# An attention stage between dense projections: where the next unit's rows are split, where dense weights are split, and which comes first where two units meet

## The chip, the cores and the metric

The kernel runs on one core of a Trainium2 chip. The metric is the device time of one execution in microseconds (us). The kernel before takes 1624.2 us, the median of three runs (1623.47 to 1624.24).

## What is computed

The reference is one inference step of a one-layer encoder. A prompt of 1024 rows and eight samples of 16 rows each, all of width 1024, are normalised and projected to queries, keys, values and gates. Two attention branches follow, each with 8 query heads of width 64:

```python
def band_attention(q, k, v, bias, valid, sink):
    s = jnp.einsum("bqhgd,bkhd->bhgqk", q, k).astype(jnp.float32) * (HEAD_DIM ** -0.5) + bias
    s = jnp.where(valid, s, NEG_INF)
    m = jnp.max(s, axis=-1, keepdims=True)
    ...
        p = jnp.exp(s - m)
        denom = jnp.sum(p, axis=-1, keepdims=True) + jnp.exp(sk - m)
    ...
    w = (p / denom).astype(v.dtype)
    return jnp.einsum("bhgqk,bkhd->bqhgd", w, v)
```

Branch A looks back over two chunks of 64 rows, has two key heads and a learned sink in the denominator; branch B looks back over eight chunks and has eight key heads and no sink. The sample rows attend to a cache of 128 earlier rows and to themselves. After it come the output projections, the gates, a merge projection and a gated feed-forward layer with a short causal convolution, with norms between. New keys and values are outputs as well.

## The kernel before

The program goes through stages: the input projections, the attention stage, the output projections and the merge, and the two halves of the feed-forward layer. Only the attention stage concerns the change. It is the second `with ExitStack() as ph` block of `encoder_step` (from L519), and in the trace it lies at about 295 to 580 us. Matrix products in full precision are made of three products of rounded parts: an operand x is split in a high part (ScalarE, a copy to the rounded type) and a low part (x minus the high part, on VectorE or GpSimd).

**Units.** The stage has eight units `u`, two heads each: 0 to 3 of branch A (shared keys and values, at most 256 keys a block), 4 to 7 of branch B (own keys and values, at most 640 keys a block). A unit's rows are 1152 wide (1024 of the prompt, 128 of the samples) and lie in DRAM; `fetch(u)` (L638) loads them with `rows` (L580, the DMA is L583) into one of two buffers (pool `rawp`). For a unit of branch A that is q alone; for branch B it is k, q and v. Then `q_done` (L599) and `k_done` (L610) split them by `split_rows` (L586) in two halves of 512 columns: the high part on ScalarE (L591), the low part on VectorE (L593 for k, L595 for q). `v_done` (L618) transposes v on TensorE (L625, L631), and VectorE and ScalarE copy the transposes to SBUF (L627, L629, L633). A raw buffer is free when all of its readers are done, and the next load waits for that on SP's queue.

**Steps.** A unit has five steps: prompt blocks 0 and 1, the samples, prompt blocks 2 and 3. A prompt step is `scores` (L670): six pairs of matmuls and more (L697, tile `s`, the two heads on two halves of TensorE's rows), a reduction with the bias and the minimum (L700, VectorE), Exp with its sum (L705, ScalarE), a reciprocal (L718) and the norms (L722, VectorE). The step after it runs `transposes` of its probabilities (L739, tile `pt` in PSUM; the copies `pk` are L741 on VectorE and L743 on ScalarE, by turns) and then `values` (L754, tile `o`; copied by L756 to `oo`, stored by L757). A sample step has its own scores (L783, L784, tile `sss`), reduction (L791), norms (L799, and L802 into `pm`), transposes (L810, L811, tile `ts`), a copy `pcs` (L813) and values (L820, L825). So at each moment a step's scores stand beside the transposes of the step before; where units meet, the scores of block 0 of unit u stand beside the transposes of block 3 of unit u − 1.

**Dense work between.** TensorE is filled up with dense projections: ten weight tiles (`dense_tiles`), each of three groups of 24 matmuls of 128x384 (L117 to L119 in `mm3`, tile `d`), copied by ScalarE to `gt` (L574) and stored (L575). `weight_tile` (L106) loads a tile's weights (L108) and splits them: high part on ScalarE (L101), low part on GpSimd (L104).

**Order.** The program is traced step by step; `spread` (L861) puts pieces of the dense work between the items of a step:

```python
items = [step(sc), step(tr, 2), step(tr, 2), rest(sc), step(tr, 2), rest(tr), lates]
```

`sc` are the scores, `tr` the transposes of the step before, `lates` the transposes of the samples' results (L833). The `fetch` of the next unit is traced ahead of the sample step (`i == 2`). A scheduler then sets the order on each engine, which is near to the order of tracing but not the same. PSUM has three pools of two buffers each: `d`; the scores and sample scores; and all the transposes together with `o`. A transpose therefore waits for the copy of the tile two before it.

Of the kernel before, what the change touches and what calls it, by code (L numbers as in the profile page):

```python
# [13 lines left out]
AF = mybir.ActivationFunctionType  # L14
ALU = mybir.AluOpType
# [12 lines left out]
GW = T // NG  # L28
# [24 lines left out]
def encoder_step(ctx, tc, x, w_in, w_o, w_out, w_upg, w_down, kc, vc, state_conv, conv_w, conv_b,  # L53
                 sink, sink_rows, t5t, onehot, relrev, g_pre_mix, g_post_mix, g_pre_ffn, g_post_ffn,
                 y, ka_new, va_new, kb_new, vb_new, conv_new):
    nc = tc.nc
# [49 lines left out]
    def weight_tile(src, name, hi_engine="scalar", lo_engine="gpsimd"):  # L106
        raw = wr.tile([P, KD, P], F32, name=f"{name}r", tag="wr")
        nc.sync.dma_start(raw[:], src)  # L108
        sp = ws.tile([P, 2, KD, P], F32R, name=f"{name}s", tag="ws")
        split_w(raw, sp, hi_engine, lo_engine)  # L110
        return sp
# [51 lines left out]
    with ExitStack() as ph:  # L163
# [100 lines left out]
        with ExitStack() as pre:  # L264
# [12 lines left out]
            for tb in range(NT):  # L277
# [3 lines left out]
                if tb == 1:  # L281
                    box = wraw.tile([P, 2, KD, P], F32, name="iwh0", tag="uw")
# [236 lines left out]
    with ExitStack() as ph:  # L519
# [35 lines left out]

        def dense_pieces(col):

            box = {}

            def run(g):  # L560
                if g == 0:
                    box["w"] = weight_tile(w_in[col], f"w{col}")
                w, c = box["w"], slice(g * GW, (g + 1) * GW)
                ps = psd.tile([P, GW], F32, name=f"d{col}_{g}", tag="d")
                for k in range(0, KD, 2):
                    mm3(ps[:], w, [xk[k // 4][:, j, :, c] for j in range(2)], k % 4, 2, start=k == 0,
                        stop=k == KD - 2, wk0=k)
                    if k < KD - 2:
                        yield
                gt = gst.tile([P, GW], F32, name=f"gt{col}_{g}", tag="gt")  # L570
                if col == dense_tiles[-1] and g == NG - 1:
                    nc.vector.tensor_copy(gt[:], ps[:])
                else:
                    nc.scalar.activation(gt[:], ps[:], AF.Copy)  # L574
                nc.sync.dma_start(in_dr[col][:, c], gt[:])  # L575
                yield

            return [lambda g=g: run(g) for g in range(NG)]
# [57 lines left out]
        def fetch(u):  # L636

            un = units[u]  # L638
            if u < 4:
                if u == 0:  # L640
                    rows(4, "ka", k_done(shared_a, "a", ka_new, 896))
                rows(u, f"q{u}", q_done(un, u))
            else:
                p = u - 4
                rows(10 + p, f"k{u}", k_done(un, f"{u}", kb_new[p], 512))
                rows(6 + p, f"q{u}", q_done(un, u))
                rows(14 + p, f"v{u}", v_done(un, f"{u}", vb_new[p], 512))

        def kv(u):
            return shared_a if u < 4 else units[u]  # L650
# [19 lines left out]
        def scores(st, u, sb):  # L670

            un, k = units[u], kv(u)
            st.name, st.u, st.sb = f"{u}_{sb}", u, sb
            nb = 2 if u < 4 else 5
            w = nb * P
            if sb == 0:
                un.bt = [setup_head(u, h) for h in range(2)]
            st.m = sm.tile([P, 2, 2, 2], F32, name=f"m{st.name}", tag="m")
            st.d = sm.tile([P, 2, 2], F32, name=f"dn{st.name}", tag="dn")
            st.p, st.k0 = [], []  # L680
            for i in range(2):
                j = 2 * sb + i
                kb = min(j + 1, nb)
                k0 = j + 1 - kb
                n = kb * P
                nch = 2 if n > 512 else 1
                cw = n // nch
                p = [pp.tile([P, 640], F32, name=f"p{st.name}_{i}_{h}", tag="p", bufs=8) for h in range(2)]
                least = [nsink[:, head_id(u, h):head_id(u, h) + 1] if u < 4 else BIG for h in range(2)]
                for c in range(nch):  # L690
                    ps = pss.tile([P, 2, 512], F32, name=f"s{st.name}_{i}_{c}", tag="s")
                    ks = slice(k0 * P + c * cw, k0 * P + (c + 1) * cw)
                    qs = slice(j * P, (j + 1) * P)
                    for t, (a, b) in enumerate(((0, 0), (1, 0), (0, 1))):
                        for h in range(2):
                            r = slice(h * HD, (h + 1) * HD)
                            nc.tensor.matmul(ps[:, h, 0:cw], un.q[a][r, qs], k.k[b][r, ks], start=t == 0, stop=t == 2)  # L697
                    for h in range(2):
                        m = st.m[:, c, h, i:i + 1]
                        nc.vector.tensor_tensor_reduce(p[h][:, c * cw:(c + 1) * cw], ps[:, h, 0:cw],  # L700
                                                       un.bt[h][:, w - n + c * cw:w - n + (c + 1) * cw], 1.0,
                                                       least[h], ALU.add, ALU.min, m)
                        least[h] = m
                for h in range(2):
                    nc.scalar.activation(p[h][:, 0:n], p[h][:, 0:n], AF.Exp, bias=least[h], scale=-1.0,  # L705
                                         accum_out=st.d[:, h, i:i + 1])
                st.p.append(p)
                st.k0.append(k0)
                if i == 0 and nch > 1:
                    yield  # L710
            yield
            if u < 4:
                e = sm.tile([P, 2, 2], F32, name=f"se{st.name}", tag="se")
                for h in range(2):
                    hid = head_id(u, h)
                    nc.scalar.activation(e[:, h], st.m[:, 0, h], AF.Exp, bias=sinkb[:, hid:hid + 1])
                nc.vector.tensor_tensor(st.d[:], st.d[:], e[:], op=ALU.add)
            nc.vector.reciprocal(st.d[:], st.d[:])  # L718
            for i in range(2):
                n = (2 * sb + i + 1 - st.k0[i]) * P  # L720
                for h in range(2):
                    nc.vector.tensor_scalar(st.p[i][h][:, 0:n], st.p[i][h][:, 0:n], st.d[:, h, i:i + 1], None,  # L722
                                            op0=ALU.mult)

        def transposes(st):

# [113 lines left out]

            later.append(late)

        later = []
        dense_tiles = [12, 16, 8, 13, 17, 9, 24, 32, 25, 33]
        pieces = []
        for col in dense_tiles:
            pieces += dense_pieces(col)

# [22 lines left out]
        for u in range(8):  # L871
            n = pieces_per_unit[u]
            dense, pieces = pieces[:n], pieces[n:]
            quanta = 4 * len(dense)
            dense = stream(dense)
            order = [("p", 0), ("p", 1), ("s", None), ("p", 2), ("p", 3)]
            share = [3, 5, 8, 12, 16] if u < 4 else [3, 6, 9, 13, 17]
            done = 0
            for i, (kind, sb) in enumerate(order):
                st = Step()  # L880
                st.kind = kind
                if i == 2 and u < 7:
                    fetch(u + 1)
                if u == 0 and i == 1:
                    rows(5, "va", v_done(shared_a, "a", va_new, 896))
                sc = scores(st, u, sb) if kind == "p" else sample_scores(st, u)
                tr = iter(())
                if prev is not None:
                    tr = transposes(prev) if prev.kind == "p" else sample_transposes(prev)

                def step(it, n=1):
                    return lambda: [next(it, None) for _ in range(n)]

                def rest(it):
                    return lambda: [None for _ in it]

                def lates():
                    for f in later:
                        f()
                    later.clear()  # L900

                items = [step(sc), step(tr, 2), step(tr, 2), rest(sc), step(tr, 2), rest(tr), lates]
                upto = quanta * share[i] // share[-1]
                spread(items, dense, upto - done)
                done = upto
                if prev is not None:
                    values(prev) if prev.kind == "p" else sample_values(prev)
                prev = st
            for _ in dense:
                pass  # L910
# [117 lines left out]
    with ExitStack() as ph:  # L1028
# [89 lines left out]
        for i, tb in enumerate(order):  # L1118
            g, c = tb // 3, (tb % 3) * P
# [12 lines left out]
            st = xp.tile([P, 4], F32, name=f"str{tb}", tag="st")  # L1132
# [240 lines left out]
    with ExitStack() as ph:  # L1373
# [167 lines left out]
        box = {"n": 0}  # L1541
# [15 lines left out]
        for g in range(2):  # L1557
# [39 lines left out]
            p5, n, _ = stepper("p5", pairs, xb, ex, False, True)  # L1597
# [4 lines left out]
            p3, n, _ = stepper("p3", pairs, xb, ex, False, False, True)  # L1602
# [94 lines left out]
```

## Time and profile before

| | |
|---|---|
| median of three runs | 1624.2 us |
| profiled execution | 1624.3 us |
| its span on the chip | 1622.5 us |
| TensorE's granted clock over the span | 0.998 |
| input projections, 0 to 294.7 us: TensorE busy | 284.52 us |
| attention stage, 294.7 to 580 us: TensorE busy | 277.41 of 285.3 us |
| the same: VectorE, ScalarE, GpSimd busy | 205.80, 163.65, 33.81 us |
| after 580 us: TensorE busy | 1024.78 of 1042.5 us |

The profile comes from one execution. PE is TensorE, PEld its loads of weights, DVE VectorE, ACT ScalarE, POOL GpSimd, SP the queue that issues the DMAs. A row of the timeline has the start, the duration, the engine, the line, the operation, what it writes and reads, and how many instructions the row holds; in brackets is the idle time of the engine ahead of it, and what released it. A duration of several instructions goes from the start of the first to the end of the last.

### The profile page before, as it was taken

The numbers are of one execution on the slowest core, as the hardware profiler recorded it, in microseconds if no ns is written. First come the engines' busy times: TensorE is split into PE (matmuls) and PEld (weight loads), VectorE is DVE, ScalarE is ACT, GpSimd is POOL, SyncE is SP. The second block draws the span as 40 slices with busy tenths as digits, with TensorE's granted clock in tenths as the row PEclk, the third lists the DMA queues.
The fourth block names the chain that finished last, engine by engine and source line by source line (L and its number), as shares of the span: only waits on it lengthen the run. The fifth ranks groups of instructions, "written<-read, shape, count | busy, mean of one in ns | idle before, by whom it ended". The sixth has DMA issues, their size and how long they took to land.

```text
span 1622.5 us, 27938 instructions
## 1 busy us (share of the span) xinstructions
PE 1586.7 (98%) x10891; PEld 1465.6 (90%) x10891; DVE 1104.8 (68%) x2055; ACT 726.9 (45%) x1428; POOL 213.5 (13%) x287
## 2 busy tenths in 40 slices
PE   8999999999999999999999999999999999999998
PEld 6999999878788789988798999999999998888886
DVE  6976544677677755453499866676666767955987
ACT  7521233666555554332463344444444445434353
POOL 1000000211110003410002211221111211000002
PEclk9999999999999999999999999999999999999999
DMA  8654321754443265352155322122221218053023
GB/s 277 212 184 151 111 102 63 232 174 153 152 155 120 63 198 174 117 204 91 65 179 147 105 69 82 56 82 79 71 82 61 77 63 357 1 217 114 1 83 151
DMA packets 93045, 205.94 MB, mean 127 GB/s; under 512 B 19321, under 2 KB 42793, under 8 KB 92914
## 3 DMA queue, kind: packets, MB, share of 16 engines
q1 hardware_dynamic: 92640, 203.35, 36.6%
q8 instruction: 85, 1.39, 0.4%
q0 software_dynamic: 272, 0.81, 0.1%
q14 instruction: 46, 0.38, 0.1%
q10 hardware_dynamic: 2, 0.00, 0.0%
HBM read 147.61 MB, written 61.24 MB: 129 GB/s over the span
## 4 chain that ended last, share of the span: by engine, by line
PE 84%; DVE 6%; ACT 4%; DMA 3%; issue 2%; SPq 0%; POOL 0%; DVEq 0%; POOLq 0%; ACTq 0%
PE x L143 17%; PE z L143 8%; PE x L1479 8%; PE ix L143 7%; PE p L1479 6%; PE iz L143 4%; PE y L143 4%; PE o L754 2%; PE r L1127 2%; PE r L1129 2%; PE r L1128 2%; PE mp L965 2%; PE mp L967 2%; PE mp L966 2%; PE d L117 2%; PE d L119 2%
## 5 line engine op out<-in xcount | busy, mean ns | idle before, releaser
L143 PE MATMUL x<-xot,s 128*128 128x288 f32 x1152 | 158.2, 295 | 2.8 <-DVE s L1084 1.6
L143 PEld LDWEIGHTS x<-xot,s 128*128 128x128 f32 x1152 | 155.0, 188 | 3.4 <-DVE s L1084 1.9
L1479 PE MATMUL x<-wbp,zap 128*128 128x512 f32 x576 | 135.3, 389 | 0.0
L1479 PEld LDWEIGHTS x<-wbp,zap 128*128 128x128 f32 x576 | 108.1, 188 | 22.4
L1083 ACT ACTIVATE s<-uw 128x512 fp32r<-128x512 f32 x96 | 60.2, 627 | 102.7 <-issue 41.7
L705 ACT ACTIVATE p<-p,m 128x256 f32<-128x256 f32 (+4 forms) x128 | 74.8, 586 | 59.5 <-DVE m L700 59.5
L1479 PE MATMUL p<-wbp,zap 128*128 128x512 f32 x432 | 100.6, 389 | 0.0
L1479 PEld LDWEIGHTS p<-wbp,zap 128*128 128x128 f32 x432 | 81.0, 188 | 17.1 <-ACT yacc L1489 0.3
L1284 DVE SCALAR_TENSOR_TENSOR wk<-w,cw,wk 128x448 f32<-128x448 f32 (+1 forms) x144 | 86.2, 635 | 2.1 <-ACT wk L1282 1.2
L1084 DVE TENSOR_TENSOR s<-uw,s 128x512 fp32r<-128x512 f32 x96 | 66.8, 697 | 28.4 <-ACT s L1083 28.1
L1084 DVE TENSOR_TENSOR a<-uw,a 128x512 fp32r<-128x512 f32 x62 | 42.9, 692 | 62.7 <-ACT a L1083 61.5
L143 PE MATMUL z<-xot,a 128*128 128x288 f32 x576 | 80.9, 295 | 0.6 <-DVE a L1084 0.6
L143 PE MATMUL x<-xob,s 128*128 128x288 f32 x576 | 81.0, 295 | 0.3 <-DVE wk L1243 0.3
L143 PE MATMUL z<-xot,s 128*128 128x288 f32 x576 | 80.7, 295 | 0.0
L143 PEld LDWEIGHTS z<-xot,a 128*128 128x128 f32 x576 | 78.1, 188 | 0.9 <-DVE a L1084 0.9
L143 PEld LDWEIGHTS x<-xob,s 128*128 128x128 f32 x576 | 78.1, 188 | 0.7 <-DVE wk L1243 0.6
L143 PE MATMUL ix<-t,s_i 128*128 128x256 f32 (+1 forms) x576 | 78.1, 294 | 0.0
L143 PEld LDWEIGHTS z<-xot,s 128*128 128x128 f32 x576 | 78.1, 188 | 0.0
L143 PEld LDWEIGHTS ix<-t,s_i 128*128 128x128 f32 x576 | 76.7, 187 | 0.0
L176 ACT ACTIVATE s_i<-iw 128x512 fp32r<-128x512 f32 x48 | 30.0, 630 | 84.2 <-PE ix L143 40.7
L739 PE MATMUL pt<-ident,p 128*128 128x128 f32 x360 | 56.9, 282 | 8.4 <-ACT pk L743 5.5
L143 PE MATMUL x<-xob,a 128*128 128x288 f32 x456 | 63.9, 295 | 0.0
(638 smaller groups left out, 3838.5 us busy)
## 6 DMA issues: line engine op xcount, KB each, us to landing
uw<-in_w_upg SPq DMA_DIRECT2D x53, 512.0 KB, 3.7
iw<-in_w_in SPq DMA_DIRECT2D x24, 512.0 KB, 3.8
gg<-in_dr SPq DMA_DIRECT2D x16, 576.0 KB, 3.7
z_dr<-wk SPq DMA_DIRECT2D x23, 256.0 KB, 2.1
in_dr<-gt SPq DMA_DIRECT2D x30, 192.0 KB, 1.9
z_dr<-wk SPq DMA_DIRECT2D x23, 224.0 KB, 1.9
xt<-in_x SPq DMA_DIRECT2D x9, 512.0 KB, 7.8
oT<-o_dr SPq DMA_DIRECT2D x8, 576.0 KB, 5.1
```

What stands on the lines that cost most here:

```text
L117: nc.tensor.matmul(ps, w[:, 0, a], xg[0][:, b], start=start and k == 0, stop=False)
L119: nc.tensor.matmul(ps, w[:, 1, a], xg[0][:, b], start=False, stop=stop and k == nk - 1)
L143: nc.tensor.matmul(ps, w[:, i, k], right(j, c, k), start=first and n == 0, stop=last and n == len(todo) - 1, skip_group_check=True)
L705: nc.scalar.activation(p[h][:, 0:n], p[h][:, 0:n], AF.Exp, bias=least[h], scale=-1.0, accum_out=st.d[:, h, i:i + 1])
L739: nc.tensor.transpose(pt[:, h * nb + b], st.p[i][h][:, c:c + P], ident[:])
L754: nc.tensor.matmul(ps[r, c], k.vs[:, kb, r], p[h], start=n == 0, stop=n == len(st.pv) - 1)
L965: nc.tensor.matmul(ps[:], self.sp[:, 0, k], oT[k][:, 0, c], start=k % 4 == 0, stop=False)
L966: nc.tensor.matmul(ps[:], self.sp[:, 0, k], oT[k][:, 1, c], start=False, stop=False)
L1083: split["left"] = nc.scalar.activation(sp[:, 0], src, AF.Copy)
L1084: split["low"] = nc.vector.tensor_tensor(sp[:, 1], src, fr(sp[:, 0]), op=ALU.subtract)
L1284: nc.vector.scalar_tensor_tensor(out, src(t), cw[:, f, t:t + 1], out, op0=ALU.mult, op1=ALU.add)
L1479: nc.tensor.matmul(ps, z[:, i, k, c], w[:, j, k], start=first and n == 0, stop=last and n == 2, skip_group_check=True)
```

## The change

There are three edits, all in the attention stage. No instruction is added or left out.

1. `dense_pieces`: the weights of a dense tile are loaded and split where group 2 of the tile before it is traced, and no longer where its own group 0 is. The first tile's weights are traced ahead of all units.
2. The `fetch` of the next unit is traced at the same place, but inside `tc.issue_after` of two instructions: on ScalarE its instructions stand behind the last Exp of step 1, on VectorE behind the last norm of step 1. Both are recorded in the dictionary `scored`.
3. Where units meet (`i == 0`, for u from 1 to 4) the first two items change places: two transposes of the unit before are traced ahead of the first scores.

```diff
         def dense_pieces(col):
 
-            box = {}
-
             def run(g):
-                if g == 0:
-                    box["w"] = weight_tile(w_in[col], f"w{col}")
-                w, c = box["w"], slice(g * GW, (g + 1) * GW)
+                if g == 2:
+                    following = dense_tiles[dense_tiles.index(col) + 1:]
+                    if following:
+                        dense_w[following[0]] = weight_tile(w_in[following[0]], f"w{following[0]}")
+                w, c = dense_w[col], slice(g * GW, (g + 1) * GW)
...
                 for h in range(2):
-                    nc.scalar.activation(p[h][:, 0:n], p[h][:, 0:n], AF.Exp, bias=least[h], scale=-1.0,
-                                         accum_out=st.d[:, h, i:i + 1])
+                    scored["high"] = nc.scalar.activation(p[h][:, 0:n], p[h][:, 0:n], AF.Exp, bias=least[h], scale=-1.0,
+                                                          accum_out=st.d[:, h, i:i + 1])
...
-                    nc.vector.tensor_scalar(st.p[i][h][:, 0:n], st.p[i][h][:, 0:n], st.d[:, h, i:i + 1], None,
-                                            op0=ALU.mult)
+                    scored["low"] = nc.vector.tensor_scalar(st.p[i][h][:, 0:n], st.p[i][h][:, 0:n], st.d[:, h, i:i + 1],
+                                                            None, op0=ALU.mult)
...
-        later = []
+        later, scored = [], {}
         dense_tiles = [12, 16, 8, 13, 17, 9, 24, 32, 25, 33]
         pieces = []
+        dense_w = {dense_tiles[0]: weight_tile(w_in[dense_tiles[0]], f"w{dense_tiles[0]}")}
...
                 if i == 2 and u < 7:
-                    fetch(u + 1)
+                    with tc.issue_after(scored["high"].ins), tc.issue_after(scored["low"].ins):
+                        fetch(u + 1)
...
                 items = [step(sc), step(tr, 2), step(tr, 2), rest(sc), step(tr, 2), rest(tr), lates]
+                if i == 0 and 0 < u < 5:
+                    items[0], items[1] = items[1], items[0]
```

## The prediction

> **What bounds the kernel now.** The page comes first: its top line, the engines' busy time and the chain that ended last.
>
> ```profile
> span 1622.5 us, 27938 instructions
> ...
> PE 1586.7 (98%) x10891; PEld 1465.6 (90%) x10891; DVE 1104.8 (68%) x2055; ACT 726.9 (45%) x1428; POOL 213.5 (13%) x287
> ...
> PE 84%; DVE 6%; ACT 4%; DMA 3%; issue 2%; SPq 0%; POOL 0%; DVEq 0%; POOLq 0%; ACTq 0%
> ```
>
> TensorE is the bound: 35.8 us of the whole span are not matmul. The change touches only the attention stage, so the windows (20 us each, 295 to 575 us) and TensorE's waits in that stage come next.
>
> ```profile
> 395.00:415.00 20.00, 17.60 (x151) 15.07 (x150) 15.20 (x51) 11.68 (x39) 4.52 (x7) 1.00 0.50 148
> ...
> sum 280.00, PE 272.11 PEld 226.37 DVE 201.28 ACT 160.92 POOL 33.81; mean PE 19.44 PEld 16.17 DVE 14.38 ACT 11.49 POOL 2.41
> ```
>
> ```profile
> PE pt L739 <- ACT pk L743: 2.7, 6, 0.7
> PE pt L739 <- DVE pk L741: 2.4, 1, 2.4
> PE o L754 <- ACT pk L743: 1.3, 3, 0.6
> ```
>
> The second column is TensorE's busy time. Only 7.9 us of the 280 are idle, and one window holds 2.4 of them. So the change can win some 8 us in this stage, and whatever it adds to TensorE's own stream is paid in full. The waits are on copies out of PSUM ahead of transposes. The timeline shows them where unit 1 meets unit 2 (PE row, and what released it):
>
> ```profile
> 352.30 0.60 PE L739 MATMUL pt<-ident,p 128*128 128x128 f32 x4
> ...
> 352.69 0.40 ACT L705 ACTIVATE p<-p,m 128x128 f32<-128x128 f32 x1 [0.96 <-DVE m L700]
> ...
> 353.47 0.57 ACT L743 ACTIVATE pk<-pt 128x512 f32<-128x512 f32 x1
> ...
> 354.10 0.44 PE L739 MATMUL pt<-ident,p 128*128 128x128 f32 x2 [0.67 <-ACT pk L743]
> ```
>
> The first transposes are done at 352.9, but their copy stands behind two Exps on ScalarE and starts at 353.47; the last pair waits 0.67 for the PSUM tile. Units 0/1 and 2/3 meet in the same way. Where 3 and 4 meet it is worse:
>
> ```profile
> 410.11 2.68 POOL L104 TENSOR_TENSOR w9s<-w9r,w9s 128x1024 fp32r<-128x1024 f32 x1 [1.27 <-issue]
> ...
> 413.26 0.28 DVE L700 CUSTOM_DVE_ANT_0 p<-s,bt 128x128 f32<-128x128 f32 x1
> ...
> 414.84 0.44 PE L739 MATMUL pt<-ident,p 128*128 128x128 f32 x2 [2.40 <-DVE pk L741]
> ...
> 416.04 1.41 PE L754 MATMUL o<-pk,vsa 128*64 128x256 f32 x12 [0.59 <-ACT pk L743]
> ```
>
> ```profile
> L595 DVE SCALAR_TENSOR_TENSOR q4l<-q4raw,q4h x2: 692/692/693, 375.3 to 379.3; 128x512 fp32r<-128x512 f32 x2
> L595 DVE SCALAR_TENSOR_TENSOR q5l<-q5raw,q5h x2: 682/1782/2882, 409.9 to 410.5; 128x512 fp32r<-128x512 f32 x2
> ```
>
> (minimum, median, maximum in ns). One half of q5l takes 2.88 us, from 410.5 to 413.3, instead of 0.69; GpSimd's w9s runs from 410.11 to 412.79. Everything behind it on VectorE starts at 413.26: unit 4's reductions, then the copy that the transposes wait for. By the Trainium skill ("SBUF — State Buffer", section "SBUF: two separate sides"), a VectorE operation with two SBUF inputs and a GpSimd one that reads SBUF exclude each other for a whole instruction; this row fits that. After the gap the granted clock (the figure before the last two) falls:
>
> ```profile
> 416.00:417.00 1.00, 0.96 (x10) 0.82 (x12) 0.76 (x4) 0.25 (x1) 0.00 (x0) 0.83 0.91 349
> 417.00:418.00 1.00, 1.00 (x10) 0.67 (x8) 0.42 (x1) 0.00 (x0) 0.00 (x0) 0.50 1.05 424
> 418.00:419.00 1.00, 1.00 (x10) 0.90 (x8) 0.25 (x1) 0.00 (x0) 0.00 (x0) 0.50 0.98 393
> 419.00:420.00 1.00, 1.00 (x7) 0.35 (x4) 0.80 (x4) 0.58 (x2) 0.00 (x0) 0.50 0.94 353
> ```
>
> That costs 0.17 + 3 × 0.5 = 1.7 us more.
>
> **The change, part by part.** Weight tiles (traced at group 2 of the tile before): ScalarE's halves L101 keep their places in its order; on GpSimd w9s and w32s only pass some memsets and a kn copy. I cost it at nothing; no wait for weights is in the list above.
>
> The swap shows on TensorE where units 1 and 2 meet (u=2's names; p_3 and pt_3 are unit 1's last step, the last number is a serial). Before:
>
> ```order
> L697 MATMUL s_0_1_0_4165<-kal,q2h 128x256 x2
> L739 MATMUL pt_3_6_4176<-ident,p_3_0_0_4050 128x128
> L739 MATMUL pt_3_6_4176<-ident,p_3_1_0_4063 128x128
> L739 MATMUL pt_3_6_4176<-ident,p_3_0_1_4051 128x128
> L739 MATMUL pt_3_6_4176<-ident,p_3_1_1_4064 128x128
> L739 MATMUL pt_3_5_4183<-ident,p_3_0_0_4050 128x128
> ```
>
> After:
>
> ```order
> L739 MATMUL pt_3_6_4145<-ident,p_3_1_1_4069 128x128
> L697 MATMUL s_0_0_0_4169<-kah,q2h 128x128
> L739 MATMUL pt_3_5_4152<-ident,p_3_0_0_4055 128x128
> L739 MATMUL pt_3_5_4152<-ident,p_3_0_1_4056 128x128
> L697 MATMUL s_0_0_0_4169<-kah,q2h 128x128
> ```
>
> The transposes now precede the scores, so their copies precede the Exps, and eleven score matmuls cover the copy: the three waits of 0.67 go (−2.0). One matmul of a pair now stands alone between transposes.
>
> Where 3 and 4 meet, on VectorE (p_0 are unit 4's first probabilities). Before:
>
> ```order
> L756 COPY oo_2_5044<-o_2_5037 128x256
> L595 SCALAR_TENSOR_TENSOR q5l<-q5raw,q5h 128x512 x2
> L700 ISA p_0_0_0_5057,m_0_5055<-s_0_0_0_5059,bt_0_5047 128x128
> L700 ISA m_0_5055 128x1
> L700 ISA p_0_0_1_5058,m_0_5055<-s_0_0_0_5059,bt_1_5051 128x128
> ```
>
> After:
>
> ```order
> L756 COPY oo_2_5049<-o_2_5042 128x256
> L741 COPY pk_3_5_5060<-pt_3_5_5059 128x256
> L700 ISA p_0_0_0_5074,m_0_5072<-s_0_0_0_5076,bt_0_5064 128x128
> L700 ISA m_0_5072 128x1
> L700 ISA p_0_0_1_5075,m_0_5072<-s_0_0_0_5076,bt_1_5068 128x128
> ```
>
> q5l is gone to unit 4's sample step and what meets w9s now reads PSUM, so 2.40 + 0.59 of idle time and the 1.7 of low clock go: −4.7. Three smaller waits stand later. Two are for ScalarE's copies, which came late behind k6, q6 and k7, q7, split at the ends of units 4 and 5 before and in their middle after:
>
> ```profile
> 455.91 0.66 PE L739 MATMUL pt<-ident,p 128*128 128x128 f32 x4 [0.27 <-ACT pk L743]
> ...
> 498.97 0.66 PE L739 MATMUL pt<-ident,p 128*128 128x128 f32 x4 [0.28 <-ACT pk L743]
> ...
> 529.52 0.79 PE L739 MATMUL pt<-ident,p 128*128 128x128 f32 x3 [0.34 <-DVE p L722]
> ```
>
> The third waits on VectorE's norms, which stand behind a copy for the output projection (L941) before and ahead of it after. All three go: −0.9. The gains sum to 2.0 + 4.7 + 0.9 = 7.6.
>
> What it adds on TensorE. In units 3 to 6 the next unit's v transposes fall among split scores (unit 4, after):
>
> ```order
> L697 MATMUL s_2_0_1_5373<-k4h,q4l 128x320 x2
> L625 MATMUL vt_0_5233<-ident,v5raw 128x128 x4
> L625 MATMUL vt_1_5239<-ident,v5raw 128x128 x4
> L697 MATMUL s_2_0_1_5373<-k4l,q4h 128x320 x2
> L631 MATMUL vt_s<-ident,v5raw 128x128
> ```
>
> Before, the v transposes stood at the first sample scores. Over the stage the order counts 27 more changes between tilings (154 to 181) and 10 more split pairs. A change's price is a run's first pair of scores against the next:
>
> ```profile
> 357.05 0.39 PE L697 MATMUL s<-kah,q2h 64*128 64x256 f32 x2
> ...
> 357.28 0.28 PE L697 MATMUL s<-kah,q2l 64*128 64x256 f32 x2
> ...
> 357.39 0.28 PE L697 MATMUL s<-kal,q2h 64*128 64x256 f32 x2
> ```
>
> 0.23 against 0.11: 0.12 for a change, and 0.11 for the second slot of a split pair. 27 × 0.12 + 10 × 0.11 = +4.3. The bounds are 0 (some changes fall in waits) and 5.5.
>
> Waits it adds. The sample step's reductions (L791) now stand behind the next unit's q halves on VectorE. The last pm pieces of units 1 and 2 against the transposes that need them (pm's four pieces in one row, from the first's start to the last's end):
>
> ```profile
> 337.15 0.94 DVE L802 TENSOR_SCALAR pm<-ps,dns 32x16 f32<-32x16 f32 x4
> ...
> 340.49 0.27 PE L811 MATMUL ts<-ident,pm 128*128 128x128 f32 x1
> ...
> 366.96 0.94 DVE L802 TENSOR_SCALAR pm<-ps,dns 32x16 f32<-32x16 f32 x4
> ...
> 368.64 0.27 PE L811 MATMUL ts<-ident,pm 128*128 128x128 f32 x1
> ```
>
> In unit 2 the slack is 368.64 − 367.90 = 0.74, and two halves of q3l take 1.3 (0.69 each, overlapping a little): a wait of 0.5. In unit 1 the slack is 340.49 − 338.09 = 2.4. There the reductions stood ahead of four norms of step 1 and o_0's copy before, and stand behind them and q2l after: 1.1 + 0.4 + 1.3 = 2.8, so 0.4 of wait. k4l's halves leave the same step, which could give that back. Together +0.9, between 0 and 2. In units 3 to 6 the sample transposes move later in TensorE's order too, behind the v transposes, so I put nothing there.
>
> The raw loads: v5raw now waits on SP's queue for the slot that k5's second half frees. Their times to landing:
>
> ```profile
> L583 SPq DMA_DIRECT2D v5raw<-in_dr x1: 320/320/320, 409.5 to 409.5; - x1
> ...
> DMA to landing us min/median/max: 3.7/4.2/5.6
> ```
>
> The copy of o out of PSUM, and two dense matmuls in a row:
>
> ```profile
> 409.51 0.42 DVE L756 COPY oo<-o 128x256 f32<-128x256 f32 x1
> ```
>
> ```profile
> 354.55 0.34 PE L118 MATMUL d<-xk,w8s 128*128 128x384 f32 x1
> ...
> 354.73 0.34 PE L119 MATMUL d<-xk,w8s 128*128 128x384 f32 x1
> ```
>
> In unit 4 the slot is free some 1.2 us after o_0 ends (its copy 0.42, then the second half of k5l 0.69). From o_0 to vt_0 TensorE has sixteen sample scores, 18 dense matmuls and five pairs of scores: about 0.9 + 18 × 0.17 + 1.0 = 5.0 us. A landing at 4.2 makes it wait 1.2 + 4.2 − 5.0 = 0.4, with the queue 0.5; at 3.7 nothing, at 5.6 1.9. For v4 to v7: 4 × 0.5 = +2.0, between 0 and 7.6. Behind vt_0 queue the transposes of the last step.
>
> **The sum**: −7.6 + 4.3 + 0.9 + 2.0 = −0.4. The profiled run took 1624.3, 0.1 above the median of 1624.2; so 1623.8. A measurement can tell 0.2%, 3.2 us.
>
> **The rivals.** *Faster, 1618.9 (0.30)*: waits stay hidden, since dense matmuls reach over them, and only half the changes cost: −7.6 + 2.2 = −5.4. For it: the 2.4 us of unit 1's slack, and the 3.7 of the quickest load. Against: TensorE is busy 97% in the stage and hides nothing of its own.
>
> *Slower, late raw loads, 1629.4 (0.15)*: v4 to v7 land after 5.6 us, as the slowest did: 4 × 1.4 more than forecast. TensorE begins to wait above 3.8 us to landing (1.2 + 3.8 = 5.0), and the sum is over 0.2% slower above 5.1. For it: two raw loads and two stores of raw rows now follow each other closely on that queue. Against: the median is 4.2.
>
> *Slower, full drains, 1629.7 (0.08)*: each change of tiling lets the matmul in flight end, 0.34 for a dense one, not 0.12: 27 × 0.22 = +5.9. The Trainium skill ("TensorEngine Tiling (Array Packing)", section "Key Properties") says that changing the tiling mode drains TensorE. The rows of 357.05 show that a change is not free, but at a third of that price.
>
> That the change does nothing is out for two parts of three, as the rows of order show; the weight part is that case.
>
> **How the numbers follow.** Forecast 0.47, within 3.2 us either way; faster 0.30; slower 0.15 + 0.08 = 0.23. The range takes the faster case's 1618.9 and the late loads' 1629.4, rounded outward.
>
> **What would show it.** Right: no idle over 0.3 us at the four meetings of units, q5l's halves both at 0.7, granted clock 1.00 from 410 to 425, VectorE's pm releasing ts in units 1 and 2, DMA v raw releasing vt in units 3 to 6. Wrong: an idle stretch over 1 us anywhere else in the stage, another VectorE operation beside GpSimd's L104 stretched to over 2 us, or score runs that begin at 0.11.

## The result, and the profile after

The changed kernel takes 1634.3 us (median of six runs, 1633.5 to 1638.9), the kernel before 1624.2 in the same runs: a ratio of 1.0065 (95% interval 1.0049 to 1.0082). That is 10 us slower, where 1623.8 us with a range to 1629.5 had been forecast.

The page first, as before: the span, TensorE, and the chain.

```profile
span 1637.2 us, 27945 instructions
...
PE 1597.5 (98%) x10891; PEld 1471.6 (90%) x10891; DVE 1105.7 (68%) x2055; ACT 727.7 (44%) x1428; POOL 213.3 (13%) x287
...
PE 84%; DVE 5%; ACT 3%; DMA 2%; issue 1%; POOL 0%; DVEq 0%; SPq 0%; POOLq 0%; ACTq 0%
```

TensorE's busy time rose by 10.8 us for the same 10891 matmuls: much of the loss is not idle time but slower matmuls. The spans themselves can't be subtracted. This execution took 1638.9 us, and 4.2 us of its excess lie at 68 to 76 us and 1.6 at 824 us, outside the attention stage: a wait of 3.4 us on ScalarE in the input projections (1.4 before), and a wait of 1.9 us that both kernels have in the feed-forward part, were each followed by a stretch at half clock here. So what follows goes by the stage: from its first dense matmul to the start of the last dense group it takes 308.8 us, against 300.4 before, 8.4 more. Of these, 7.0 are busy time of TensorE (the first figure behind the comma; the kernel before first):

```profile
294.83:595.25 300.42, 289.71 (x2511) 241.12 (x2510) 213.25 (x754) 169.93 (x478) 33.81 (x51) 0.99 0.45 144
```

```profile
299.04:607.88 308.84, 296.68 (x2512) 243.95 (x2510) 213.91 (x754) 170.48 (x478) 33.51 (x51) 0.99 0.43 140
```

TensorE's waits in the stage:

```profile
PE vt L625 <- DMA v7raw<-in_dr: 2.3, 1, 2.3
PE o L754 <- ACT pk L743: 2.0, 3, 0.7
PE vt L625 <- DMA v5raw<-in_dr: 1.6, 1, 1.6
PE vt L625 <- DMA v6raw<-in_dr: 1.4, 1, 1.4
PE pt L739 <- DVE vs L627: 1.3, 1, 1.3
PE pt L739 <- ACT pk L743: 1.3, 5, 0.4
```

The wait of 2.4 us on VectorE's copy where units 3 and 4 meet is gone. In its place TensorE waits three times for v's raw rows, and once for the copy of v's transposes.

**Unit 4, where v5 comes late.** The timeline of TensorE, VectorE and SP's queue, from the norms of step 1 on:

```profile
426.58 1.54 DVE L722 TENSOR_SCALAR p<-p,dn 128x384 f32<-128x384 f32 x4
...
426.99 0.87 PE L754 MATMUL o<-pk,vs 128*64 128x256 f32 x8
...
428.64 0.41 DVE L756 COPY oo<-o 128x256 f32<-128x256 f32 x1
428.98 0.68 DVE L593 TENSOR_TENSOR k5l<-k5raw,k5h 128x512 fp32r<-128x512 f32 x1
...
429.69 0.32 SPq L583 DMA_DIRECT2D v5raw<-in_dr  x1
...
434.46 0.76 PE L625 MATMUL vt<-ident,v5raw 128*128 128x128 f32 x5 [1.62 <-DMA v5raw<-in_dr]
```

o_0 ends at 427.86, but the norms run to 428.12, and k5's low half, held behind them, ends at 429.66. Only then is the slot free and the load issued; it lands 4.7 us later.

**Unit 5, where a tiny operation takes 2.3 us.** GpSimd's split of a weight tile, and pm's last four pieces on VectorE:

```profile
478.85 2.36 POOL L104 TENSOR_TENSOR w32s<-w32r,w32s 128x1024 fp32r<-128x1024 f32 x1 [20.82 <-ACT w32s L101]
478.91 3.10 DVE L802 TENSOR_SCALAR pm<-ps,dns 32x16 f32<-32x16 f32 x4
479.57 1.09 PE L625 MATMUL vt<-ident,v6raw 128*128 128x128 f32 x8 [1.40 <-DMA v6raw<-in_dr]
...
482.87 0.69 DVE L627 COPY vs<-vt 128x512 f32<-128x512 f32 x1
...
483.61 0.66 PE L739 MATMUL pt<-ident,p 128*128 128x128 f32 x4 [1.32 <-DVE vs L627]
```

Four pieces of pm take 0.94 elsewhere; here they take 3.10. VectorE comes late to v6's transposes, and they hold the PSUM tile that TensorE wants. Then the clock, in windows of 1 us (the figure before the last two):

```profile
485.00:486.00 1.00, 0.70 (x5) 0.44 (x4) 0.10 (x1) 1.00 (x3) 0.00 (x0) 0.80 0.94 384
486.00:487.00 1.00, 1.00 (x6) 0.72 (x4) 0.00 (x0) 0.54 (x3) 0.03 (x1) 0.50 0.24 55
487.00:488.00 1.00, 1.00 (x7) 0.62 (x8) 0.44 (x2) 0.39 (x1) 0.92 (x2) 0.50 0.02 2
488.00:489.00 1.00, 1.00 (x6) 0.62 (x8) 0.89 (x4) 0.00 (x0) 0.10 (x1) 0.50 0.00 0
...
530.00:531.00 1.00, 1.00 (x5) 0.72 (x5) 0.93 (x2) 0.23 (x1) 0.00 (x0) 0.50 0.74 275
531.00:532.00 1.00, 1.00 (x5) 0.90 (x5) 0.70 (x4) 0.96 (x2) 0.00 (x0) 0.50 0.16 23
532.00:533.00 1.00, 1.00 (x6) 1.00 (x5) 0.00 (x0) 0.34 (x3) 0.00 (x0) 0.50 0.18 26
533.00:534.00 1.00, 1.00 (x7) 0.80 (x5) 0.37 (x1) 1.00 (x2) 0.00 (x0) 0.80 0.96 283
```

Twice TensorE runs at half clock, 1.7 us lost each time: after the waits of unit 5 and after the 2.3 us of unit 6.

**Units 1 to 3, where the swap gives little.** The three waits of 0.67 where units meet are gone, and three of 0.65 to 0.67 stand at o_0, a step later, where there was none in unit 1 before and 0.33 and 0.34 in units 2 and 3. So 0.7 us of waits are won, not 2.0. Unit 2 before, and unit 1 after:

```profile
360.92 0.87 PE L754 MATMUL o<-pk,vsa 128*64 128x256 f32 x8 [0.33 <-ACT pk L743]
```

```profile
333.14 0.39 PE L697 MATMUL s<-kah,q1h 64*128 64x256 f32 x2
...
336.69 0.57 ACT L743 ACTIVATE pk<-pt 128x512 f32<-128x512 f32 x1
...
337.32 0.87 PE L754 MATMUL o<-pk,vsa 128*64 128x256 f32 x8 [0.65 <-ACT pk L743]
```

From the first score of block 1 to o_0 it is 337.32 − 333.14 = 4.18 us. Before it was 333.25 − 329.07 = 4.18 as well: the chain through the reductions, four Exps and the copy behind them has its own length, and what TensorE does not fill of it, it waits. (In units 2 and 3 the chain grew from 3.87 to 4.20: VectorE's reductions begin 1.0 us after the first score and no longer 0.67, since the norms of the step before and o's copy, which stand ahead of them, end later.)

The table puts it together: us between the first scores of block 1 in one unit and in the next, read from the timelines (the last line but one from unit 7 to the start of the last dense group), for the two kernels and for the ten of the next section.

| | before | after | e1 | e2 | e3 | e4 | e5 | e6 | e7 | e8 | e9 | e10 |
|---|---|---|---|---|---|---|---|---|---|---|---|---|
| unit 1 to 2 | 28.0 | 28.6 | 28.6 | 28.3 | 28.6 | 28.6 | 28.7 | 28.6 | 28.0 | 28.0 | 28.7 | 28.0 |
| 2 to 3 | 28.1 | 28.6 | 28.4 | 28.2 | 28.6 | 28.6 | 28.6 | 28.6 | 28.1 | 28.1 | 28.6 | 27.8 |
| 3 to 4 | 32.2 | 31.3 | 31.7 | 30.7 | 31.2 | 31.0 | 31.2 | 30.7 | 29.4 | 30.0 | 31.0 | 29.7 |
| 4 to 5 | 44.2 | 45.3 | 43.0 | 47.0 | 46.9 | 43.3 | 47.0 | 48.6 | 43.4 | 43.0 | 43.4 | 43.4 |
| 5 to 6 | 43.1 | 48.5 | 43.1 | 47.3 | 43.1 | 43.3 | 44.9 | 50.4 | 43.0 | 43.0 | 43.3 | 43.3 |
| 6 to 7 | 44.1 | 48.1 | 43.9 | 47.7 | 44.0 | 47.7 | 46.1 | 46.4 | 44.3 | 44.0 | 45.6 | 46.5 |
| 7 to the end | 46.5 | 44.3 | 46.0 | 45.1 | 47.8 | 43.9 | 46.0 | 44.6 | 44.6 | 44.6 | 44.3 | 49.3 |
| whole stage | 300.4 | 308.8 | 299.0 | 308.3 | 304.2 | 300.4 | 306.4 | 311.8 | 295.2 | 295.4 | 299.1 | 302.4 |

Units 5 and 6 lose 5.4 and 4.0 us: all of the loss and more. The stage end wins 2.2, which the moved pieces don't explain: before, a copy for the last transposes stood on ScalarE behind a split that waited for its load; in the later stage of the changed kernel it had landed. (In e8, which moves nothing there, the row is 44.6 as well.) Before:

```profile
587.42 1.16 ACT L940 ACTIVATE oT<-oT 128x1152 fp32r<-128x1152 f32 x1 [2.62 <-DMA oT<-o_dr]
588.49 0.58 ACT L743 ACTIVATE pk<-pt 128x512 f32<-128x512 f32 x1
...
589.12 0.44 PE L739 MATMUL pt<-ident,p 128*128 128x128 f32 x2 [2.31 <-ACT pk L743]
```

A second table divides the same stage: TensorE's idle time, what the clock took (half of each stretch at 0.50), the rest of the stage against the kernel before, and how many more changes of tiling TensorE's instructions make (157 before, counted in the trace; the prediction's counts start from 154, the expectations' from 151, with the same differences).

| us | before | after | e1 | e2 | e3 | e4 | e5 | e6 | e7 | e8 | e9 | e10 |
|---|---|---|---|---|---|---|---|---|---|---|---|---|
| idle | 10.7 | 12.2 | 8.4 | 11.5 | 9.1 | 9.5 | 11.2 | 9.4 | 6.9 | 7.3 | 7.9 | 10.5 |
| clock | 1.7 | 3.4 | 0 | 5.1 | 3.4 | 0 | 1.7 | 8.5 | 0 | 0 | 0 | 3.4 |
| rest, more than before | 0 | 5.3 | 2.5 | 3.6 | 3.6 | 2.9 | 5.5 | 5.8 | 0.3 | 0.0 | 3.2 | 0.5 |
| changes, more than before | 0 | 27 | 13 | 15 | 19 | 13 | 26 | 37 | 0 | 0 | 13 | −1 |

So of the 8.4 us, waits are 1.5 and the clock is 1.7, both net of what was won, and 5.3 are matmuls that take longer at full clock. This rest follows the cutting of TensorE's stream in all kernels: 0.16 to 0.24 us for each change more where there are any, and 0.5 or less in all where there are none (e7, e8, e10).

### The profile page after: what moved, and what is told of

The parts are those of the page before. It is cut to its first block, busy times and chain, and to the rows that moved or that the text cites. A ratio compares the mean times of both kernels' runs of the same rounds, so it can differ in the third digit from the quotient of the medians.

```text
span 1637.2 us, 27945 instructions
## 1 busy us (share of the span) xinstructions
PE 1597.5 (98%) x10891; PEld 1471.6 (90%) x10891; DVE 1105.7 (68%) x2055; ACT 727.7 (44%) x1428; POOL 213.3 (13%) x287
## 4 chain that ended last, share of the span: by engine, by line
PE 84%; DVE 5%; ACT 3%; DMA 2%; issue 1%; POOL 0%; DVEq 0%; SPq 0%; POOLq 0%; ACTq 0%
PE x L143 17%; PE z L143 8%; PE ix L143 8%; PE x L1483 8%; PE p L1483 6%; PE iz L143 5%; PE y L143 4%; PE pt L739 2%; PE r L1131 2%; PE o L754 2%; PE r L1133 2%; PE r L1132 2%; PE mp L970 2%; PE mp L971 2%; PE mp L969 2%; PE s L697 2%
## 5 line engine op out<-in xcount | busy, mean ns | idle before, releaser
L1088 DVE TENSOR_TENSOR s<-uw,s 128x512 fp32r<-128x512 f32 x96 | 66.8, 697 | 28.4 <-ACT s L1087 28.1
L143 PE MATMUL y<-xob,a 128*128 128x288 f32 x456 | 63.9, 295 | 0.0
```

Of the source, the lines that this page charges most:

```text
L143: nc.tensor.matmul(ps, w[:, i, k], right(j, c, k), start=first and n == 0, stop=last and n == len(todo) - 1, skip_group_check=True)
L1088: split["low"] = nc.vector.tensor_tensor(sp[:, 1], src, fr(sp[:, 0]), op=ALU.subtract)
```

## Experiments

**Undo the hold.** `fetch(u + 1)` loses its two `issue_after`. The weights and the swap stay. (The weights alone change no engine's order: instruction for instruction it is that of the kernel before. So this is also the swap by itself.)

```diff
-                    with tc.issue_after(scored["high"].ins), tc.issue_after(scored["low"].ins):
-                        fetch(u + 1)
+                    fetch(u + 1)
```

> The changed kernel with the hold taken back: the next unit's rows are loaded and split where the scheduler puts them, as before; the weights and the swap stay. Theory A (the hold makes v's raw rows land late and sets the sample step's VectorE work beside a weight split on GpSimd; each wait of over a microsecond then costs a stretch at half clock): the 10 us are gone, and the three waits of 0.67 us where units meet stay away, so 1621 to 1624 us, with no wait of TensorE on v raw in units 4 to 6. Rival B (the swap and the finer cutting of TensorE's stream cost the time): 1630 us or more, since the swap is still there. Changes of tiling in the stage: 164 against 151 before and 178 after.

Measured: ratio to before 0.9999 (0.9990 to 1.0009), medians 1625.4 and 1625.0. TensorE's waits in the stage, and q5's low halves:

```profile
PE o L754 <- ACT pk L743: 3.4, 4, 1.6
PE pt L739 <- ACT pk L743: 2.6, 5, 1.0
```

```profile
L595 DVE SCALAR_TENSOR_TENSOR q5l<-q5raw,q5h x2: 681/1782/2882, 411.5 to 412.1; 128x512 fp32r<-128x512 f32 x2
```

No wait on v, and the 10 us are gone: the loss comes with the hold. But the swap brings no gain, where 1621 to 1624 had been expected. q5's half still takes 2.88 us, and its wait moved from the transposes to o (1.6 of the 3.4 us). Rival B is out as the main cause, but not without a part: what the hold adds to e1's stage is 3.7 us of waits, 3.4 of clock and 2.7 of the rest, with 14 changes of tiling more.

**The hold alone**, without swap and weights.

```diff
-                if i == 0 and 0 < u < 5:
-                    items[0], items[1] = items[1], items[0]
```

> The kernel before with the hold alone: the next unit's fetch stands behind the last Exp and the last norm of step 1; weights and swap as before. Theory A: all of the loss is here, 1633 to 1637 us, with waits on v raw of 1.4 to 2.3 us in units 4 to 6. Rival B (swap and finer cutting): 1622 to 1626 us. Changes of tiling: 166.

Measured: 1.0051 (1.0036 to 1.0066), median 1634.0, 9.0 over before: nearly the whole loss again. Its waits:

```profile
PE vt L623 <- DMA v7raw<-in_dr: 1.9, 1, 1.9
PE vt L623 <- DMA v6raw<-in_dr: 1.9, 1, 1.9
PE vt L623 <- DMA v5raw<-in_dr: 1.8, 1, 1.8
```

All three are followed by half clock here, and units 4, 5 and 6 lose 2.8, 4.2 and 3.7 us.

**The hold up to unit 5's rows** (`u < 5`); units 6 and 7 are fetched as before.

> The changed kernel with the hold for the rows of units 1 to 5 alone; units 6 and 7 are fetched as before. Theory A: what units 5 and 6 lose in the trace (5.4 and 4.0 us) comes back, 1624 to 1626 us; unit 4 still waits 1.6 us for its successor's v. Rival B: the cutting falls from 178 to 170 changes of tiling only, so 1630 to 1633 us.

Measured: 1.0020 (1.0008 to 1.0031), 1628.6 against 1625.0: 3.5 us over, where 0 to 2 had been expected. Units 5 and 6 come out as before, to 0.1 us. Most of the rest is unit 4, 2.7 us longer than before: in this execution the wait for v5 (1.7) was followed by half clock, as it wasn't in the changed kernel. The stage end is 1.3 longer, with a wait of 1.7 on ScalarE's copy and half clock.

**v ahead of k and q** in `fetch`, the hold kept.

```diff
+                rows(14 + p, f"v{u}", v_done(un, f"{u}", vb_new[p], 512))
                 rows(10 + p, f"k{u}", k_done(un, f"{u}", kb_new[p], 512))
                 rows(6 + p, f"q{u}", q_done(un, u))
-                rows(14 + p, f"v{u}", v_done(un, f"{u}", vb_new[p], 512))
```

> The changed kernel with v loaded ahead of k and q in branch B, so that v takes the slot that is free early and q takes the one that v frees. The hold stays. Theory A: no wait on v raw in units 4 to 6, so 1620 to 1625 us, if q's load, now last, lands before its split is due; where it does not, ScalarE or VectorE wait for q instead and the time is 1628 us or more. Rival B: 164 changes of tiling, like the kernel without the hold, so it does not tell B from A alone.

Measured: 1.0012 (0.9994 to 1.0030), 1627.5 against 1625.0, short of the 1620 to 1625 expected. No wait on v is left, and units 4 and 5 are within 0.3 us of the best. Unit 6 still takes 47.7 us, and its timeline shows a cause:

```profile
511.03 2.36 POOL L104 TENSOR_TENSOR w25s<-w25r,w25s 128x1024 fp32r<-128x1024 f32 x1 [16.42 <-ACT w25s L101]
511.17 2.77 DVE L593 TENSOR_TENSOR k7l<-k7raw,k7h 128x512 fp32r<-128x512 f32 x1
...
514.59 0.44 PE L739 MATMUL pt<-ident,p 128*128 128x128 f32 x2 [1.24 <-DVE vs L627]
```

Another VectorE operation had come to stand beside another weight split. (A second wait in unit 6, 1.58 us for a copy of ScalarE's at 532 us, is 0.23 in e9, where this split is gone.)

**One weight tile's low part on VectorE**, w32 in the changed kernel.

```diff
-weight_tile(w_in[following[0]], f"w{following[0]}")
+weight_tile(w_in[following[0]], f"w{following[0]}", lo_engine="vector" if following[0] == 32 else "gpsimd")
```

> The changed kernel, but the low part of one dense weight tile, w32, is split on VectorE instead of GpSimd. Theory C (in unit 5 a piece of pm on VectorE is held for 2.3 us by GpSimd's split of w32, and so holds the copy of v's transposes and 1.3 us of TensorE): no piece of pm over 0.4 us, the wait of TensorE's transposes on vs in unit 5 gone, unit 5 shorter by 1.3 to 3 us (the upper end if the half clock of unit 5 goes too), 7 to 9 us over the kernel before in all. Rival: the wait on vs comes from v6's late landing alone, and unit 5 stays as long as it was (48.5 us).

Measured: 1.0055 (1.0037 to 1.0073), 9.2 us over before by the medians, just outside the 7 to 9. In the stage theory C holds: pm's pieces, changed kernel first,

```profile
L802 DVE TENSOR_SCALAR pm<-ps,dns x64: 212/225/2322, 314.5 to 574.2; 32x16 f32<-32x16 f32 x64
```

```profile
L803 DVE TENSOR_SCALAR pm<-ps,dns x64: 215/225/283, 310.5 to 566.0; 32x16 f32<-32x16 f32 x64
```

and unit 5 takes 44.9 instead of 48.5, with the wait for v6 (1.2) left and no half clock behind it. (The stretched pieces alone do not make TensorE wait: in e2 and e6 the same four took 3.17 and 3.06 us, and no wait on vs followed.) The other units keep their waits on v, and unit 4's was followed by half clock this time.

**v's load in two halves**, in the changed kernel.

```diff
+                nc.sync.dma_start(raw[:, 0:512], in_dr[col][:, 0:512])
+                nc.sync.dma_start(raw[:, 512:T], in_dr[col][:, 512:T])
```

> The changed kernel, with v's raw rows in branch B loaded by two DMAs (512 columns, then the rest) instead of one, so that the first transposes need the first half alone. Theory A (late landing): the waits on v raw in units 4 to 6 fall from 1.4 to 2.3 us to under 1 us each, no stretch at half clock follows them, and the kernel is 4 to 7 us faster than the changed one, 3 to 6 us over the kernel before. Rival B (the finer cutting costs the time): 188 changes of tiling and 32 lone halves against 178 and 24, so it is as slow as the changed kernel or slower, 10 us or more over the kernel before.

Measured: 1.0061 (1.0043 to 1.0079): no faster. Theory A's number was missed, though not its mechanism: the first half still lands 3.8 to 4.3 us after its issue, and the waits stayed.

```profile
PE vt L629 <- DMA v6raw<-in_dr: 1.7, 1, 1.7
PE vt L629 <- DMA v5raw<-in_dr: 1.4, 1, 1.4
PE vt L629 <- DMA v7raw<-in_dr: 1.2, 1, 1.2
```

The stage was longer than the changed kernel's by 3.0 us (311.8), with 2.8 us less waiting but 5.1 more lost to the clock: there were 6.8 us at half clock in unit 4, and in unit 5

```profile
479.00:481.00 2.00, 2.00 (x10) 1.31 (x9) 1.92 (x5) 0.60 (x1) 1.28 (x2) 0.50 0.73 282
...
485.00:487.00 2.00, 2.00 (x8) 1.69 (x8) 1.33 (x5) 0.21 (x1) 0.96 (x2) 0.50 0.11 36
487.00:489.00 2.00, 2.00 (x11) 1.25 (x11) 0.42 (x1) 2.00 (x5) 0.09 (x1) 0.58 0.00 0
```

That is 10 us at half clock, not 3.4. The number is the one that rival B gave, but not for rival B's reason: against the changed kernel the rest grew by 0.6 us only, for 10 changes more.

**Hold q5 alone**, in the kernel before: k and v as they were, no swap.

```diff
+                if u == 5:
+                    with tc.issue_after(scored["high"].ins), tc.issue_after(scored["low"].ins):
+                        rows(6 + p, f"q{u}", q_done(un, u))
+                else:
+                    rows(6 + p, f"q{u}", q_done(un, u))
```

> The kernel before, with one hold alone: q of unit 5 is split behind the last Exp and norm of unit 4's step 1; k and v of unit 5 and all other units as before; no swap, weights as before. Theory C: q5's low half no longer meets GpSimd's split of w9, so the 2.4 and 0.6 us of idle time and the half clock where units 3 and 4 meet are gone, and v5 takes its slot as early as before: 3.5 to 5 us faster than the kernel before. Rival: the reductions there are late for another reason, and an idle stretch of over a microsecond stays between 410 and 418 us; no faster than before.

Measured: 0.9978 (0.9968 to 0.9989), 1621.3 against 1625.3: 4 us faster than the kernel before, as expected. q5's halves take 0.68 each, and no wait of TensorE in the stage is over 0.7:

```profile
PE pt L743 <- ACT pk L747: 3.9, 8, 0.7
PE o L758 <- ACT pk L747: 0.7, 2, 0.3
```

```profile
L595 DVE SCALAR_TENSOR_TENSOR q5l<-q5raw,q5h x2: 680/682/683, 420.7 to 421.6; 128x512 fp32r<-128x512 f32 x2
```

**w9's low part on VectorE**, in the kernel before, nothing moved.

> The kernel before, but the low part of one dense weight tile, w9, is split on VectorE instead of GpSimd; nothing else moves. Theory C: q5's low half takes 0.7 us again instead of 2.9. VectorE does the split of w9 itself, some 1.2 us, so about half of the idle time where units 3 and 4 meet is gone, and with it the half clock, if the wait falls under about 1.4 us: 2.5 to 4.5 us faster than before. Rival: q5's half is slow for another reason, such as its operands; it stays at 2.9 us and the time does not change.

Measured: 0.9979 (0.9969 to 0.9990), 1621.9 against 1625.3. q5's half is quick in its old place:

```profile
L595 DVE SCALAR_TENSOR_TENSOR q5l<-q5raw,q5h x2: 681/684/686, 412.0 to 412.6; 128x512 fp32r<-128x512 f32 x2
```

So it was GpSimd's split that held it, and neither the operation nor its operands. TensorE waits 1.2 us there, as expected, and keeps its clock.

**v first, and w25's low part on VectorE.**

> The changed kernel with v loaded ahead of k and q (as in e4_v_first), and the low part of weight tile w25 split on VectorE instead of GpSimd. In e4 the waits on v raw were gone, but unit 6 still took 47.7 us: one half of k7's low part ran beside GpSimd's split of w25 and took 2.8 us instead of 0.7. Theory C: that was unit 6's whole loss, so unit 6 takes 44 to 45 us, the stage 296 to 298 us, and the kernel is 1 to 4 us faster than the kernel before. Rival: unit 6 loses to the later q or to the cutting, and stays over 46.5 us; no faster than before.

Measured: 1.0005 (0.9992 to 1.0018), medians 1626.2 and 1625.6: not faster, against the 1 to 4 us expected. In the profiled execution unit 6 falls from 47.7 to 45.6 (44 to 45 expected) and the stage to 299.1 (296 to 298). So the lock was most of unit 6's loss, not all of it. The other 1.5 us are 1.0 of small waits, the longest 0.63 on VectorE's pk, and 0.5 of the rest, with two changes of tiling more; where those waits come from was not found.

**Hold q in all of branch B**, the kernel before otherwise.

> The kernel before, with q alone held behind the last Exp and norm of step 1 for units 4 to 7; k and v as before, no swap. Theory A (the hold costs because v's load waits for the slot of a held k): no wait on v raw, the time like e7_hold_q5_alone, 3 to 5 us faster than the kernel before, unless a held q meets a weight split. Rival D (splits set ahead of the sample step's reductions cost time of their own, by late sample transposes): units 5 and 6 are each over 0.5 us longer than before.

Measured: 0.9987 (0.9976 to 0.9999), 1624.0 against 1625.6. No wait on v, as theory A says, and units 4 and 5 are 43.4 and 43.3, 0.2 over before in unit 5: rival D is out there. But 1.6 us faster is less than the 3 to 5: q7's low half now met w25's split,

```profile
L595 DVE SCALAR_TENSOR_TENSOR q7l<-q7raw,q7h x2: 684/1730/2776, 506.7 to 507.6; 128x512 fp32r<-128x512 f32 x2
```

unit 6 lost 2.4 us, and the stage end had 2.1 us of wait and half clock.

## Why the prediction was wrong

*v's loads, +2.0.* It came 3.3 us short. The waits were 0, 1.62, 1.40 and 2.25, 5.3 together. The prediction let the slot be free 1.2 us after o_0; it was 1.8, since step 1's norms, which the hold sets ahead of k's split, were still running when o_0 ended. And it took the median landing of before, 4.2, where these loads took 4.5 to 5.4. The rival of late loads had the right place, with 0.15. Its waits, 7.6, were above the 5.3 measured; what it lacked is the clock and the lock below.

*The clock.* The prediction counted the half clock as a gain where units 3 and 4 meet, and did not charge it to any wait that the change adds. It cost 2 × 1.7 in the changed kernel. With it the rival of late loads would have reached 1633 us.

*The lock.* The row of q5l and w9 was read rightly (e7, e8), and the prediction named a stretched operation beside L104 as a sign of being wrong. But it costed the weights at nothing because their order does not move. What moved was VectorE's work past them: the sample step's pm, later by the splits set ahead of it, met w32. That cost a wait of 1.3 us, one of 0.3 right behind it, and its part in a half clock; e5 shows it.

*The swap, −2.0.* The waits went as said, but "eleven score matmuls cover the copy" was the wrong place to stop. The next thing late was o_0, 4.18 us after step 1's first score in unit 1 of both kernels. The prediction's own list had it: of its three waits of o on pk, 1.3 together, two stand there. In e1, which is the swap alone, units 1 to 3 come out 0.9 us longer, not 2.0 shorter: the waits are 0.2 less, and the rest is 1.1 more with seven changes of tiling.

*Where units 3 and 4 meet, −4.7.* Right in mechanism. e7 shows it by itself: 2.8 and 0.8 us from the two rows that hold it, 3.6.

*The smaller waits, −0.9.* Two of the three only fell by 0.1 each, so −0.5.

*Cutting, +4.3.* About right, and in size the largest loss with v's waits: the rest of the stage grew by 5.3, within the bounds of 0 to 5.5, and did so in step with the changes of tiling from kernel to kernel. The rivals that changed this term, half the cost (2.2) and full drains (10.2), are out. The page of the Trainium skill ("TensorEngine Tiling (Array Packing)", section "Key Properties") gives the drain no price; here a change, lone halves of pairs included, came to some 0.2 us.

*Sample chain, +0.9.* About right in size, 0.2 on pm and 0.5 on the copy behind it, but not in place: the wait on pm is unit 0's, and in units 1 and 2 the transposes do not wait for pm.

In the stage that leaves −0.7 (swap), −4.7, −0.5, +5.3 (cutting), +0.7 (sample chain), +5.3 (v), +1.6 (lock), +3.4 (clock) and −2.0 (waits at the stage end, not forecast): 8.4, against −0.4 forecast. The steps that failed are the clock and the lock, put at nothing (5.0 together), v's waits at 2.0 instead of 5.3, and the swap at −2.0 instead of −0.7; the stage end, by luck, took 2.0 back. The medians differ by 10.1. Where the other 1.7 lie stays open: the stage's lengths are of one execution each, and from one execution to another a stretch at half clock comes or goes.

## What to carry to other kernels

Holding work back on one engine also holds the buffers that it reads, and so the next load: follow the slot to the queue, to the landing and to whoever waits there, before calling the hold free. Price a wait of TensorE with the half clock that may follow it, not with its length alone. Count how often the new order changes TensorE's tiling, since that is paid even where nothing waits. When an operation is moved on VectorE, look at what GpSimd runs at its new place, not only at the old one; here the one good piece of the change was to part two such operations, and doing that alone (e7 or e8) is 0.2% faster than the kernel before.

## What the runs showed of the hardware

In these rows a VectorE operation between SBUF tiles that started while a GpSimd split ran lasted until the split's end, whatever its size: 32x16 in 2.32 us instead of 0.22, and 128x512 in 2.8 to 2.9 instead of 0.69, while copies and reductions out of PSUM beside the same splits kept their time. This fits the lock of the Trainium skill ("SBUF — State Buffer", section "SBUF: two separate sides"), which has it for two SBUF inputs and for VectorE's modes with two ports; the 32x16 piece has a single tensor input and a column of scalars, and no row here shows its mode. Beside q7l in the changed kernel, whose first half had begun 0.31 us earlier, it was the split that took longer, 3.23 us instead of 2.37.

The clock halved after waits of 1.4 to 2.3 us and not only after long ones. Of the waits on v in these runs all of 1.8 us and more were followed by it; of those between 1.2 and 1.7 some were and some were not, the same one in the same unit among them (unit 4's: 1.62 without, 1.7 with). Length alone does not decide: the kernel before waited 2.31 us at the stage end and kept its clock, and a wait of 1.9 us in the feed-forward part, which all twelve profiles have, was followed by half clock in seven of them. A stretch lasted 3.4 us in most cases, 7 us in three places and 10 in one (e6). The Trainium skill ("TensorE: Matmul & The Clock Gate", section "Part 1: The HAM clock gate (the "warmup" mystery)") has the clock fall after an idle window of about 3.4 us that runs freely; the length of the stretches agrees, and the waits that sufficed here are half as long.
